# A hybrid attention and state-space layer on one core: the states' scans in two steps, their rotation back on GpSimd, the phasors as two rows with the third negated by ScalarE

## The chip, the cores and the metric

The kernel runs on 1 core of one Trainium2 chip. The metric is device microseconds from start to end of one execution, the median of several runs. Engines are named as the profile names them: PE is TensorE (matmul; PEld its weight loads), DVE is VectorE, ACT is ScalarE, POOL is GpSimd, SP is SyncE, which issues most DMAs here.

## The reference

One layer on 2048 positions of width 1024, in float32. Two branches share one input projection: latent attention (4 heads), and a bidirectional S5 state-space branch, 32 groups of 16 channels with 64 complex states in each direction. The part that matters here, cut:

```python
lam_bar = jnp.exp(lam * dt)
b_bar = ((lam_bar - 1.0) / lam)[..., None] * b
bu = jnp.einsum('sbgh,gph->sbgp', u_c, b_bar)
a = jnp.broadcast_to(lam_bar, (seq, 1, SSM_GROUPS, SSM_STATE))
_, h = lax.associative_scan(_diag_scan_op, (a, bu), reverse=reverse, axis=0)
y = y + jnp.real(jnp.einsum('sbgp,ghp->sbgh', h, c))
...
s = jnp.einsum('bqhd,bkhd->bhqk', qn, k_nope) + jnp.einsum('bqhr,bkr->bhqk', qr, k_rope)
p = jax.nn.softmax(s * scale, axis=-1)
return jnp.einsum('bhqk,bkhd->bqhd', p, v)
```

After that: GELU and a gated linear unit on the S5 branch, a norm and a gate on both, one output projection, a norm and the residual.

## The kernel before

Phase 1 projects the input, phase 3 does the output side. Between them lies the attention phase, in which all of S5 runs too; the change touches that phase alone. It is one hand-written loop (`for t in range(8 * NU + LAG + AVLAG + 3)`) of 256 steps with scores and a short tail. All five engines are scheduled by hand: each engine executes its instructions in exactly the order in which this loop emits them, and an instruction that waits holds everything behind it on its engine.

One step of attention: five score matmuls of 512 columns (L1103 to L1107, into `sc`, two PSUM buffers); the row maximum `nm` on DVE (L1108); the exponential `e` on ACT (L1114); the scaling of an older `e` on ACT (`norm`, L1143); four transposes of an older `e` on PE (`pt`, L1151), split into `phi` on ACT (L1159) and `plo` on DVE (L1573); and six matmuls with the values on the `phi` and `plo` of the step before (`av`, L1171 to L1173). Every eight steps a unit (128-query pairs, one head) ends, with some small statistics on DVE.

S5 runs group by group: `group(g)` is a generator that does one piece before and one after the attention's part of each step. A new group starts every 7 steps (twice 6), and each takes 15, so that two or three are under way. In this text a **round** is the 7 steps from the start of one group, and **offsets** 0 to 6 count its steps. At offset o the new group does its step o, and the group before it does its step 7 + o; of step 14, at offset 0, there is the older one's end. By a group's own steps, before the change:

- steps 0 and 1: the table `w` on POOL (L905, L906, L961). Step 2: `t3`, the phasors over the chunks as three rows (-sin, cos, sin), as two products on POOL, `t` and `t3b` (L971, L972); step 3: their sum (L975), then transposes of `w` on PE, split by ACT and DVE (`wTh`, `wTl`).
- step 5: matmuls `px`. Step 6: `ta` and `tb` on DVE from `px` and the phasors (L996, L997). Step 7 (offset 0 of the next round): `X`, their sum (L1001).
- step 8 (offset 1): four scans on DVE, real and imaginary part, forward and backward (L1008, L1009), from `X` into `G`.
- step 9 (offset 2): the rotation back: `hc`, a product on DVE (L1017), and `tb2`, shown as `tb`, a product on POOL (L1018).
- step 10 (offset 3): their difference, again `hc`, on DVE (L1021).
- step 14 (offset 0): `hc` goes into matmuls.

What shares POOL's queue in a round: three instructions of a table `v` for a later four groups (L905, L906, L915), in some rounds a split of inputs (`ul` L883, `ml` L889, which wait for ACT), and `qd` of the next queries (L750), which waits for DVE.

Of the kernel before, what the change touches and what calls it, by code (L numbers as in the profile page):

```python
# [11 lines left out]
F32 = mybir.dt.float32  # L12
# [4 lines left out]
ALU = mybir.AluOpType  # L17
# [4 lines left out]
P = 128  # L22
# [34 lines left out]
class Metered:  # L57
    """An engine that counts the elements it is given."""
# [13 lines left out]
class Scratch:  # L72
    """Temporaries of one shape, out of a ring of tiles of 512 (or, if small, 32) elements."""
# [10 lines left out]
def reduce_angle(eng, sc, out, ang):  # L84
    """out = ang - 2 pi round(ang / 2 pi)."""
    k = sc()
    eng.tensor_scalar(k, ang, 1.0 / TWO_PI, MAGIC, ALU.mult, ALU.add)
    eng.tensor_scalar(k, k, MAGIC, None, ALU.subtract)
    yield
    eng.scalar_tensor_tensor(out, k, -PI_1, ang, ALU.mult, ALU.add)  # L90
    for c in (PI_2, PI_3, PI_4):
        yield
        eng.scalar_tensor_tensor(out, k, -c, out, ALU.mult, ALU.add)
    yield


def sincos(eng, sc, sin_out, cos_out, r):
    """sin and cos of r in about [-pi, pi], from those of r / 2."""
    z, a = sc(), sc()
    eng.scalar_tensor_tensor(z, r, 0.25, r, ALU.mult, ALU.mult)  # L100
    s = [(-1.0) ** n / math.factorial(2 * n + 1) for n in range(1, 7)]
    eng.tensor_scalar(a, z, s[5], None, ALU.mult)
    for c in s[4::-1]:
        yield
        eng.scalar_tensor_tensor(a, a, c, z, ALU.add, ALU.mult)
    yield
    s2 = sc()
    eng.scalar_tensor_tensor(s2, a, 1.0, r, ALU.add, ALU.mult)
    c = [(-1.0) ** n / math.factorial(2 * n) for n in range(1, 8)]
    eng.tensor_scalar(a, z, c[6], None, ALU.mult)  # L110
    for v in c[5::-1]:
        yield
        eng.scalar_tensor_tensor(a, a, v, z, ALU.add, ALU.mult)
    yield
    eng.scalar_tensor_tensor(sin_out, a, 1.0, s2, ALU.add, ALU.mult)
    yield
    eng.scalar_tensor_tensor(cos_out, s2, -0.5, s2, ALU.mult, ALU.mult)
    eng.tensor_scalar(cos_out, cos_out, 1.0, None, ALU.add)
    yield


def exp_of(eng, sc, pool, out, x):
    """exp(x) in float32, exact at 0."""
    xc, n, r, a = sc(), sc(), sc(), sc()
    eng.tensor_scalar(xc, x, -87.0, 88.0, ALU.max, ALU.min)
    eng.tensor_scalar(n, xc, 1.0 / math.log(2.0), MAGIC, ALU.mult, ALU.add)
    eng.tensor_scalar(n, n, MAGIC, None, ALU.subtract)
    eng.scalar_tensor_tensor(r, n, -LN2_1, xc, ALU.mult, ALU.add)
    eng.scalar_tensor_tensor(r, n, -LN2_2, r, ALU.mult, ALU.add)
    yield  # L130
    eng.tensor_scalar(a, r, 1.0 / 5040, None, ALU.mult)
    for k in (720, 120, 24, 6, 2, 1):
        eng.scalar_tensor_tensor(a, a, 1.0 / k, r, ALU.add, ALU.mult)
    eng.tensor_scalar(a, a, 1.0, None, ALU.add)
    yield
    e = pool.tile(sc.shape, I32, tag="expi", name="expi")
    eng.tensor_scalar(n, n, 127.0, None, ALU.add)
    eng.tensor_copy(e, n)
    eng.tensor_scalar(e, e, 23, None, ALU.logical_shift_left)
    eng.tensor_tensor(out, a, f32(e), ALU.mult)  # L140


def bc(ap, dims):
    return ap.to_broadcast(dims)
# [3 lines left out]
def tile_hymba(ctx, tc, x, pos, inv_freq, pre_g, w_in, q_g, w_uqT, w_uqr, kv_g, w_ukT, w_uv, attn_g,  # L148
# [35 lines left out]
    def rsqrt_of(ss, n, scale, eps=EPS):  # L184
        """(ss * scale + eps) ** -0.5 on [128, n]."""
        v = sm.tile([P, n], F32, tag=f"rv{n}", name="rv")
        r = sm.tile([P, n], F32, tag=f"rr{n}", name="rr")
        V.tensor_scalar(v, ss, scale, eps, ALU.mult, ALU.add)
        G.tensor_tensor(r, v, nhalf[:, :n], ALU.pow)
        return r  # L190

    def split(hi, lo, src, scale=None):
        """hi + lo = src (* a scale for each partition), both float32r."""
# [12 lines left out]
    # tables of the attention phase; those of S5 go through DRAM, by groups  # L206
# [11 lines left out]
    # ------------------------------------------------------------------ phase 1  # L218
# [51 lines left out]
    def turn(xt, t):  # L270
        """The tile's transpose, split, as tile t of a pair."""
# [34 lines left out]
    def gemm_t(nm, half):  # L306
        """Two blocks of 128 columns of a pair of tiles, with the columns in the partitions."""
# [43 lines left out]
    def s5_params():  # L351
# [37 lines left out]
        # F = (lam_bar - 1) / lam  # L389
# [17 lines left out]
        # powers of lam_bar, 0 .. T, in the order of each direction  # L407
# [29 lines left out]
        # phasors of chunk 32 i + 2 j + a: ph32 * (0..7) (+ phi), for a = 0, 1, and ph2 * (0..15)  # L437
# [13 lines left out]
        for nm, src in (("b", ph2), ("a", ph32)):  # L451
# [21 lines left out]
            # the backward direction turns the other way  # L473
# [11 lines left out]
        # B_bar = F B; B'' = B_bar e^{-i phi}; C' = lam_bar C  # L485
# [3 lines left out]
        def cm(orr, oi, ar, ai, xr_, xi_):  # L489
            """(orr, oi) = (ar + i ai)(xr + i xi), a over the last dimension."""  # L490
# [32 lines left out]
        # centre lag: Re(C B_bar) of both directions + D  # L523
        # (eight groups at a time: theirs are the blocks on the diagonal)
# [36 lines left out]
    def step():  # L561
        """A slice of the tables, of about BUDGET elements."""
# [4 lines left out]
    def blocks(s):  # L567
        """The columns of two tiles, a block of columns at a time: z goes first and last, tile by tile,
        so that the next tiles can take the places of these meanwhile."""
# [8 lines left out]
    # absorbed weights: W_uq[h] W_uk[h]^T  # L578
# [23 lines left out]
    # the first tile is loaded and normed by halves  # L602
# [48 lines left out]
    # ------------------------------------------------------------------ phase 2  # L651
    # (the gate columns of the last two tiles run under its start)
# [43 lines left out]
    # queries of a block of 256: each piece's last results are split a step later  # L696
# [74 lines left out]
    def both(*gens):  # L771
        """Step some routines in turn; what each returns."""
# [14 lines left out]
    # the gate columns of the last two tiles run under the start of the attention  # L787
# [58 lines left out]
    # S5  # L846
# [8 lines left out]
    def s5_load(q):  # L855
        """The tables of four groups."""
# [34 lines left out]
    def ops4(tile_, q_r, q_i, c1, c2):  # L891
        """The operands of tile_[., 2, s, h] = q_r[s] c1[., h] + q_i[s] c2[., h]."""
# [9 lines left out]
    def two(eng, tile_, tmp, *o):  # L902
        """The two products of a table; later they are added."""
# [18 lines left out]
    def k_build(q):  # L922
        """The kernels of the lags within a chunk, and their windows for each position."""
# [26 lines left out]
    def group(g):  # L950
        """A group of channels, a step at a time: what is ready first, what needs the PE last."""
        q, i = divmod(g, 4)
        f = S5[q]
        # (chunks in the order of their tiles: those of the even, then those of the odd places)
# [9 lines left out]
        # phasors over the chunks: -sin, cos, sin  # L964
        t3 = s2.tile([P, 3, 16, 16], F32, tag="t3", name="t3", bufs=2)
        t3b = s2.tile([P, 3, 16, 16], F32, tag="t3b", name="t3b")
        d = [P, 3, 16, 16]
# [3 lines left out]
        G.tensor_tensor(t3, bc(f["aa"][:, i, 1:4, :].unsqueeze(3), d), b4(f["bc"]), ALU.mult)  # L971
        G.tensor_tensor(t3b, bc(f["aa"][:, i, 0:3, :].unsqueeze(3), d), b4(f["bs"]), ALU.mult)  # L972
        yield "pre"
        yield "post"
        G.tensor_tensor(t3, t3, t3b, ALU.add)  # L975
# [7 lines left out]
        yield "post"  # L983
        yield "pre"
# [19 lines left out]
        # (the states that enter the chunks; nothing enters the first, or the last backwards)  # L1004
# [6 lines left out]
        yield "pre"  # L1011
        yield "post"
# [4 lines left out]
        V.tensor_tensor(of_tiles(hc), g4, co, ALU.mult)  # L1017
# [3 lines left out]
        V.tensor_tensor(hc, hc, tb2, ALU.subtract)  # L1021
        yield "pre"
        yield "post"
# [20 lines left out]
    # when each group starts; the tables of the next four groups are made meanwhile  # L1044
# [52 lines left out]
    # attention  # L1097
# [19 lines left out]
    # the blocks of a row were shifted by their own maxima: bring them to the row's, and divide  # L1117
# [67 lines left out]
    # ------------------------------------------------------------------ weights of phase 3  # L1185
# [52 lines left out]
    # ------------------------------------------------------------------ phase 3  # L1238
    # (pairs of tiles, with the channels in the partitions up to W_out)
    def mixer():  # L1240
# [26 lines left out]
        def gelu(d):  # L1267
            """y <- 2 gelu(y), and its parts"""
# [38 lines left out]
        def part(d, src, h, c):  # L1307
            """hi and lo of half h of src, as blocks c .. of the products' operands"""
# [16 lines left out]
        def summed(d, sq):  # L1325
            """The sums of squares of the four channels in a partition"""
# [5 lines left out]
        def attn(d):  # L1332
            """o gated, and its parts"""
# [16 lines left out]
        def ssm(d):  # L1350
            """y <- 4 y sigmoid(. + b), gated into g, and its parts"""
# [37 lines left out]
        # the columns of the result in the parts that are worked on; the last tile ends in smaller ones  # L1389
# [11 lines left out]
        def comb(d, t, cs):  # L1401
            """Both branches by their factors, summed; the mean of the squares; times the gain"""
# [40 lines left out]
        # the first pairs, in small steps between those of the attention  # L1443
# [103 lines left out]
    for t in range(8 * NU + LAG + AVLAG + 3):  # L1547
        n, i = divmod(t, 8)
        # what the step before has made ready
# [5 lines left out]
        # scores  # L1555
# [23 lines left out]
        # (without scores in between, its operands take a step longer)  # L1579
# [8 lines left out]
        # the queries of the next block  # L1588
# [37 lines left out]
def layout(i):  # L1626
    """The inputs, laid out for the core; nothing is computed from them."""
# [51 lines left out]
```

## Time and profile before

| | before |
|---|---|
| median of 3 runs | 1433.84 us (1433.35 to 1434.98) |
| span of the profiled execution | 1431.5 us |
| PE, DVE, ACT, POOL busy | 95%, 74%, 55%, 44% |
| PE granted clock, mean | 0.997 |

The span runs from the first to the last instruction in one profiled execution; the median lies 2.3 us above it. Busy shares are over the whole span. The attention phase is the middle of it: its first score matmul starts at 394 us, its last step's at 1168 us. PE is pipelined and the ends of its matmuls are modelled, so that busy PE time may hide short waits.

### The profile page before, as it was taken

How to read it: one execution, taken by the hardware profiler on the slowest of the kernel's cores; microseconds unless marked ns; L12 is line 12 of the kernel's file. 1: busy time of each engine (PE TensorE's matmuls, PEld its weight loads, DVE VectorE, ACT ScalarE, POOL GpSimd, SP SyncE). 2: the span in 40 equal slices, each digit the busy share in tenths (PEclk: the TensorE clock that was granted, in tenths of full speed). 3: DMA queues.
4: the chain of work that ended last, by engine and by line, in shares of the span. 5: the costliest groups of instructions: out<-in, count | busy, mean ns of one | idle time of the engine just before them, and what ended most of it. 6: DMA issues, size and time to landing. Idle time of an engine off the chain costs nothing.

```text
span 1431.5 us, 24291 instructions
## 1 busy us (share of the span) xinstructions
PE 1359.6 (95%) x9016; PEld 1221.6 (85%) x9016; DVE 1053.7 (74%) x1876; ACT 789.0 (55%) x1796; POOL 624.9 (44%) x616
## 2 busy tenths in 40 slices
PE   7999999999989999999999998999999989999998
PEld 7999999999968788887888887887888878788886
DVE  5456545332588888898989888988888895876774
ACT  6321222122457767767677676676677775544542
POOL 2102321233364655555556555645542695323340
PEclk9999999999999999999999999999999999999999
DMA  8322332442610110201102011020100345345432
GB/s 293 89 61 66 80 87 73 98 122 73 150 35 19 39 34 5 54 19 31 41 5 61 12 32 41 23 43 5 32 5 9 101 128 131 118 148 179 145 103 88
DMA packets 122133, 102.91 MB, mean 72 GB/s; under 512 B 14672, under 2 KB 107104, under 8 KB 122016
## 3 DMA queue, kind: packets, MB, share of 16 engines
q1 hardware_dynamic: 110384, 89.43, 22.3%
q0 software_dynamic: 2272, 7.62, 2.0%
q10 hardware_dynamic: 9360, 4.33, 1.5%
q8 instruction: 70, 1.15, 0.3%
q14 instruction: 47, 0.39, 0.1%
HBM read 63.80 MB, written 37.54 MB: 71 GB/s over the span
## 4 chain that ended last, share of the span: by engine, by line
PE 59%; DVE 26%; ACT 5%; issue 4%; POOL 2%; DMA 2%; SPq 1%; ACTq 0%; POOLq 0%; DVEq 0%
DVE plo L1573 5%; DVE nm L1108 4%; PE po L202 4%; PE po L203 4%; PE po L204 4%; PE pt L1151 3%; DVE hc L1017 3%; DVE G L1009 3%; DVE G L1008 3%; PE z_ga L203 2%; PE z_ga L204 2%; PE z_ga L202 2%; PE av L1173 2%; PE z_u L204 2%; PE z_u L202 2%
## 5 line engine op out<-in xcount | busy, mean ns | idle before, releaser
L1114 ACT ACTIVATE e<-sc,nm 128x512 f32<-128x512 f32 x256 | 176.4, 689 | 141.1 <-DVE nm L1108 139.8
L1573 DVE TENSOR_TENSOR plo<-pt,phi 128x512 fp32r<-128x512 f32 x255 | 175.0, 686 | 49.2 <-ACT phi L1159 46.3
L1159 ACT ACTIVATE phi<-pt 128x512 fp32r<-128x512 f32 x256 | 152.8, 597 | 72.9 <-PE pt L1151 72.4
L1108 DVE TENSOR_REDUCE nm<-sc 128x1 f32<-128x512 f32 x256 | 175.0, 683 | 17.6 <-PE sc L1107 15.6
L1173 PE MATMUL av<-plo,kn_h 128*128 128x256 f32 x512 | 150.6, 294 | 30.0 <-DVE plo L1573 29.5
L1171 PE MATMUL av<-phi,kn_h 128*128 128x256 f32 x512 | 165.7, 324 | 13.3 <-ACT avs L1176 13.2
L1143 ACT ACTIVATE e<-e,f 128x512 f32<-128x512 f32 x226 | 163.8, 725 | 1.5 <-DVE f L1132 1.5
L1151 PEld LDWEIGHTS pt<-ident,e 128*128 128x128 f32 x1024 | 127.8, 141 | 38.9 <-DVE e L1139 4.5
L1151 PE MATMUL pt<-ident,e 128*128 128x128 f32 x1024 | 154.8, 274 | 4.3 <-DVE e L1139 3.5
L1172 PE MATMUL av<-phi,kn_l 128*128 128x256 f32 x512 | 144.6, 282 | 0.0
L1173 PEld LDWEIGHTS av<-plo,kn_h 128*128 128x128 f32 x512 | 96.5, 189 | 40.1 <-DVE plo L1573 39.3
L1018 POOL TENSOR_TENSOR tb<-G,t 128x512 f32<-128x512 f32 x32 | 41.6, 1301 | 192.2 <-DVE G L1009 192.2
L1103 PE MATMUL sc<-kT_h,qo 128*128 128x512 f32 x256 | 114.7, 448 | 2.9 <-ACT e L1114 1.4
L1171 PEld LDWEIGHTS av<-phi,kn_h 128*128 128x128 f32 x512 | 97.6, 191 | 16.6 <-ACT avs L1176 16.5
L202 PE MATMUL po<-woh,ah 128*128 128x512 f32 (+1 forms) x264 | 102.6, 389 | 1.9 <-ACT u L1410 1.9
L203 PE MATMUL po<-wol,ah 128*128 128x512 f32 (+1 forms) x264 | 102.4, 388 | 0.0
L204 PE MATMUL po<-woh,al 128*128 128x512 f32 (+1 forms) x264 | 102.3, 388 | 0.0
L1104 PE MATMUL sc<-kT_l,qo 128*128 128x512 f32 x256 | 101.5, 396 | 0.0
L1106 PE MATMUL sc<-krS,qo 128*128 128x512 f32 x256 | 101.3, 396 | 0.0
L1107 PE MATMUL sc<-krS,qo 128*128 128x512 f32 x256 | 101.2, 395 | 0.0
L1105 PE MATMUL sc<-kT_h,qo 128*128 128x512 f32 x256 | 100.8, 394 | 0.0
L1172 PEld LDWEIGHTS av<-phi,kn_l 128*128 128x128 f32 x512 | 97.7, 191 | 0.0
(337 smaller groups left out, 4148.6 us busy)
## 6 DMA issues: line engine op xcount, KB each, us to landing
g_d<-gst SPq DMA_DIRECT2D x64, 128.0 KB, 2.0
g<-g_d SPq DMA_DIRECT2D x16, 512.0 KB, 5.7
xr<-in_x_dram SPq DMA_DIRECT2D x16, 512.0 KB, 6.7
xt<-in_x_dram SPq DMA_DIRECT2D x15, 512.0 KB, 3.8
out_dram<-res SPq DMA_DIRECT2D x15, 512.0 KB, 3.1
u_d<-ust ACTq DMA_DIRECT2D x64, 64.0 KB, 2.1
u<-u_d SPq DMA_DIRECT2D x64, 64.0 KB, 2.5
o_d<-o SPq DMA_DIRECT2D x32, 128.0 KB, 1.8
```

The costliest lines, as they stand in the source:

```text
L202: PE.matmul(ps, ahi, bhi, start=first, stop=False)
L203: PE.matmul(ps, ahi, blo, start=False, stop=False)
L204: PE.matmul(ps, alo, bhi, start=False, stop=last)
L1108: V.tensor_reduce(st["nm"][:, qt, kb:kb + 1], ps, AX.X, ALU.max, negate=True)
L1114: A.activation(e, st.pop("s"), AF.Exp, bias=st["nm"][:, qt, kb:kb + 1], accum_out=st["L"][:, qt, kb:kb + 1])
L1143: A.activation(e, e, AF.Copy, scale=f)
L1151: PE.transpose(pt[:, kk, qt, :], st["e"][qt, kt // 4][:, o:o + P], ident)
L1159: A.activation(hi, ptf, AF.Copy)
L1171: PE.matmul(o, kn_h[:, kt, :], hi[:, w], start=kt == 0, stop=False)
L1172: PE.matmul(o, kn_l[:, kt, :], hi[:, w], start=False, stop=False)
L1173: PE.matmul(o, kn_h[:, kt, :], lo[:, w], start=False, stop=kt == NT - 1)
L1573: V.tensor_tensor(lo[0], lo[1], f32(lo[2]), ALU.subtract)
```

## The change

In `group(g)` alone (docstrings and comments are also gone, which moves the line numbers; after the rotation back they are lower by one):

```diff
-        t3b = s2.tile([P, 3, 16, 16], F32, tag="t3b", name="t3b")
-        d = [P, 3, 16, 16]
+        t3b = s2.tile([P, 2, 16, 16], F32, tag="t3b", name="t3b")
+        d = [P, 2, 16, 16]
...
-        G.tensor_tensor(t3, bc(f["aa"][:, i, 1:4, :].unsqueeze(3), d), b4(f["bc"]), ALU.mult)
-        G.tensor_tensor(t3b, bc(f["aa"][:, i, 0:3, :].unsqueeze(3), d), b4(f["bs"]), ALU.mult)
+        G.tensor_tensor(t3[:, 0:2], bc(f["aa"][:, i, 1:3, :].unsqueeze(3), d), b4(f["bc"]), ALU.mult)
+        G.tensor_tensor(t3b, bc(f["aa"][:, i, 0:2, :].unsqueeze(3), d), b4(f["bs"]), ALU.mult)
         yield "pre"
         yield "post"
-        G.tensor_tensor(t3, t3, t3b, ALU.add)
+        G.tensor_tensor(t3[:, 0:2], t3[:, 0:2], t3b, ALU.add)
...
         split(wh_, wl_, pw[:, 0:256])
         yield "post"
+        A.activation(t3[:, 2, :], t3[:, 0, :], AF.Copy, scale=-1.0)
         yield "pre"
...
             V.tensor_tensor_scan(gt[64:P, o + 1:o + NC][:, ::-1], df[64:P], xm[64:P, r, 1:][:, ::-1], 0.0,
                                  ALU.mult, ALU.add)
-        yield "pre"
-        yield "post"
+            yield "pre"
+            yield "post"
...
-        V.tensor_tensor(of_tiles(hc), g4, co, ALU.mult)
+        G.tensor_tensor(of_tiles(hc), g4, co, ALU.mult)
         G.tensor_tensor(of_tiles(tb2), g4[:, ::-1], si, ALU.mult)
         yield "pre"
         yield "post"
-        V.tensor_tensor(hc, hc, tb2, ALU.subtract)
-        yield "pre"
-        yield "post"
+        G.tensor_tensor(hc, hc, tb2, ALU.subtract)
```

So the scans of the real part stay at step 8 and those of the imaginary part move to step 9; the rotation back moves from steps 9 and 10 to steps 10 and 11, all of it on POOL; one pair of empty yields goes, so that steps 12 to 14 stay where they were. The phasors' products have 512 elements in a partition, not 768, and ACT writes the third row at step 4.

Where this stands in the queues. First DVE, one round in the middle of the phase, from the `nm` and `plo` of offset 0 on (`G` is what the scans write; the numbers behind names tell buffers apart); before:

```order
L1108 TENSOR_REDUCE nm<-sc 128x1
L1573 TENSOR_TENSOR plo<-pt_9349,phi 128x512
L1008 SCALAR_TENSOR_TENSOR G_4637<-tab_7930,X_4639 64x255
L1009 SCALAR_TENSOR_TENSOR G_4637<-tab_7930,X_4639 64x255
L1008 SCALAR_TENSOR_TENSOR G_4637<-tab_7930,X_4639 64x255
L1009 SCALAR_TENSOR_TENSOR G_4637<-tab_7930,X_4639 64x255
L1108 TENSOR_REDUCE nm<-sc 128x1
L1573 TENSOR_TENSOR plo<-pt_9391,phi 128x512
L1017 TENSOR_TENSOR hc<-G_4637,t_9140 128x512
L1108 TENSOR_REDUCE nm<-sc 128x1
L1573 TENSOR_TENSOR plo<-pt_9426,phi 128x512
L1021 TENSOR_TENSOR hc<-hc,tb_9412 128x512
```

and the same round with the change:

```order
L1107 TENSOR_REDUCE nm<-sc 128x1
L1572 TENSOR_TENSOR plo<-pt_9366,phi 128x512
L1009 SCALAR_TENSOR_TENSOR G_4637<-tab_7942,X_4639 64x255
L1010 SCALAR_TENSOR_TENSOR G_4637<-tab_7942,X_4639 64x255
L1107 TENSOR_REDUCE nm<-sc 128x1
L1572 TENSOR_TENSOR plo<-pt_9406,phi 128x512
L1009 SCALAR_TENSOR_TENSOR G_4637<-tab_7942,X_4639 64x255
L1010 SCALAR_TENSOR_TENSOR G_4637<-tab_7942,X_4639 64x255
L1107 TENSOR_REDUCE nm<-sc 128x1
L1572 TENSOR_TENSOR plo<-pt_9439,phi 128x512
```

Two scans now stand between one `nm` and the next where there were four, and both `hc` are gone from this queue. Second POOL, from the table `w` of a new group to the end of the older group's rotation; before:

```order
L905 TENSOR_TENSOR w<-tab_7930 128x256
L906 TENSOR_TENSOR tmp<-tab_7930 128x256
L961 TENSOR_TENSOR w<-w,tmp 128x256
L1018 TENSOR_TENSOR tb_9137<-G_4638,t_8842 128x512
L971 TENSOR_TENSOR t_9140<-tab_7930 128x768
L972 TENSOR_TENSOR t3b<-tab_7930 128x768
L975 TENSOR_TENSOR t_9140<-t_9140,t3b 128x768
```

and with the change:

```order
L905 TENSOR_TENSOR w<-tab_7942 128x256
L906 TENSOR_TENSOR tmp<-tab_7942 128x256
L961 TENSOR_TENSOR w<-w,tmp 128x256
L971 TENSOR_TENSOR t_9152<-tab_7942 128x512
L972 TENSOR_TENSOR t3b<-tab_7942 128x512
L1018 TENSOR_TENSOR hc<-G_4638,t_8853 128x512
L1019 TENSOR_TENSOR tb_9191<-G_4638,t_8853 128x512
L975 TENSOR_TENSOR t_9152<-t_9152,t3b 128x512
L1022 TENSOR_TENSOR hc<-hc,tb_9191 128x512
```

The first instruction that needs the scans' result `G` stood ahead of the new group's phasors; now the two products of the phasors stand ahead of it, and behind it come one more product and one difference. Third ACT, where the negation comes in (a later group), with the change:

```order
L195 ACTIVATE wTh<-pw_10354 128x256
L1142 ACTIVATE e<-e,f 128x512
L984 ACTIVATE t_10287<-t_10287 128x256
L1158 ACTIVATE phi<-pt_10371 128x512
L1113 ACTIVATE e,L<-sc,nm 128x512
```

The row of L984 is new; it stands between the scaling of `e` and `phi` of offset 4, and it reads what POOL's sum (L975) wrote.

## Rows read from the trace of the kernel before

**Rows 1.** The page: span, and busy time of each engine over it.
```profile
span 1431.5 us, 24291 instructions
...
PE 1359.6 (95%) x9016; PEld 1221.6 (85%) x9016; DVE 1053.7 (74%) x1876; ACT 789.0 (55%) x1796; POOL 624.9 (44%) x616
```

**Rows 2.** The page: the chain of waits that ended last, shares by engine.
```profile
PE 59%; DVE 26%; ACT 5%; issue 4%; POOL 2%; DMA 2%; SPq 1%; ACTq 0%; POOLq 0%; DVEq 0%
```

**Rows 3.** Busy time by stretch: offsets 2 to 4 of 31 rounds, and their sum.
```profile
core 0: us, PE busy (x) PEld busy (x) DVE busy (x) ACT busy (x) POOL busy (x), PEclk, DMA share, GB/s
...
577.13:584.74 7.61, 7.59 (x50) 6.58 (x48) 7.15 (x10) 5.84 (x14) 7.53 (x6) 1.00 0.35 95
...
642.10:652.55 10.45, 8.12 (x53) 6.81 (x51) 9.59 (x15) 6.59 (x18) 6.51 (x4) 1.00 0.01 2
...
708.33:717.03 8.70, 8.14 (x55) 7.14 (x54) 7.98 (x17) 5.42 (x14) 6.77 (x5) 1.00 0.01 2
...
839.59:847.40 7.81, 7.81 (x54) 6.91 (x53) 6.83 (x11) 5.92 (x17) 7.73 (x6) 1.00 0.36 92
...
sum 295.50, PE 255.45 PEld 218.74 DVE 269.84 ACT 192.85 POOL 240.18; mean PE 8.24 PEld 7.06 DVE 8.70 ACT 6.22 POOL 7.75
```

**Rows 4.** The same for the four other offsets of these rounds, summed.
```profile
sum 380.10, PE 378.72 PEld 337.90 DVE 328.00 ACT 285.71 POOL 129.41; mean PE 12.22 PEld 10.90 DVE 10.58 ACT 9.22 POOL 4.17
```

**Rows 5.** Groups on DVE: count, busy us, mean ns, idle before and releaser.
```profile
L1017 DVE TENSOR_TENSOR hc<-G,t 128x512 f32<-128x512 f32 x32 | 52.3, 1635 | 0.0
L1009 DVE TENSOR_TENSOR_SCAN G<-tab,X 64x255 f32<-64x255 f32 x64 | 46.3, 724 | 0.9
L1008 DVE TENSOR_TENSOR_SCAN G<-tab,X 64x255 f32<-64x255 f32 x64 | 45.4, 709 | 0.4
L1021 DVE TENSOR_TENSOR hc<-hc,tb 128x512 f32<-128x512 f32 x32 | 41.3, 1292 | 2.5 <-POOL tb L1018 2.5
```

**Rows 6.** Timeline of DVE, 641 to 650 us: start, us, instruction.
```profile
641.83 0.69 DVE L1009 TENSOR_TENSOR_SCAN G<-tab,X 64x255 f32<-64x255 f32 x1
...
643.88 2.03 DVE L1017 TENSOR_TENSOR hc<-G,t 128x512 f32<-128x512 f32 x1
...
647.83 1.92 DVE L1021 TENSOR_TENSOR hc<-hc,tb 128x512 f32<-128x512 f32 x1
```

**Rows 7.** Timeline of POOL, the same stretch.
```profile
642.60 1.31 POOL L1018 TENSOR_TENSOR tb<-G,t 128x512 f32<-128x512 f32 x1 [10.71 <-DVE G L1009]
...
647.34 1.85 POOL L975 TENSOR_TENSOR t<-t,t3b 128x768 f32<-128x768 f32 x1
```

**Rows 8.** Timeline of DVE in another round: the product with POOL idle at its start.
```profile
710.02 0.68 DVE L1017 TENSOR_TENSOR hc<-G,t 128x512 f32<-128x512 f32 x1
```

**Rows 9.** Timeline of PE, the stretch of rows 6: idle before an instruction, and its releaser.
```profile
647.16 0.39 PE L1173 MATMUL av<-plo,kn_h 128*128 128x256 f32 x1 [0.58 <-DVE plo L1573]
...
651.48 0.39 PE L1171 MATMUL av<-phi,kn_h 128*128 128x256 f32 x1 [1.75 <-ACT avs L1176]
```

**Rows 10.** Groups on POOL.
```profile
L975 POOL TENSOR_TENSOR t<-t,t3b 128x768 f32<-128x768 f32 x32 | 63.1, 1971 | 2.2
L972 POOL TENSOR_TENSOR t3b<-tab 128x768 f32<-128x768 f32 x32 | 60.3, 1885 | 0.0
L971 POOL TENSOR_TENSOR t<-tab 128x768 f32<-128x768 f32 x32 | 48.1, 1502 | 0.0
L1018 POOL TENSOR_TENSOR tb<-G,t 128x512 f32<-128x512 f32 x32 | 41.6, 1301 | 192.2 <-DVE G L1009 192.2
```

**Rows 11.** Groups on ACT: a copy of 128x256.
```profile
L195 ACT ACTIVATE wTh<-pw 128x256 fp32r<-128x256 f32 x32 | 12.3, 384 | 0.0
```

**Rows 12.** Timeline of DVE, POOL and ACT, the round of the first stretch of rows 3.
```profile
576.30 0.69 DVE L1009 TENSOR_TENSOR_SCAN G<-tab,X 64x255 f32<-64x255 f32 x1
...
581.82 2.17 POOL L975 TENSOR_TENSOR t<-t,t3b 128x768 f32<-128x768 f32 x1
...
583.86 0.72 ACT L1143 ACTIVATE e<-e,f 128x512 f32<-128x512 f32 x1
```

**Rows 13.** Timeline of DVE and POOL, a round in which POOL's splits came late.
```profile
506.78 1.61 DVE L1009 TENSOR_TENSOR_SCAN G<-tab,X 64x255 f32<-64x255 f32 x1
...
507.80 1.69 POOL L889 TENSOR_TENSOR ml<-m,mh 128x512 fp32r<-128x512 f32 x1
```

## The prediction

> **What bounds the kernel now.** I read the page first: over the span of 1431.5 us PE is busy for 1359.6, DVE for 1053.7, POOL for 624.9 [rows 1]. PE looks like the bound; but the chain of waits lies on DVE for 26% [rows 2], so somewhere PE waits for DVE, and the question is where. The change touches the attention phase alone, so I cut that phase by rounds and asked for busy time by stretch: offsets 2 to 4, three steps that hold the rotation back, against the four other offsets, for 31 rounds. The reader should see how different the two are. Offsets 2 to 4 last 295.5 us in all with PE busy for 255.45: 40.05 us of idle PE, 1.29 a round, with DVE busy 91% and POOL 81% of it [rows 3]. The other four offsets last 380.10 us with PE busy for 378.72: 1.38 us of idle in all, POOL busy 34% [rows 4]. So nearly all the visible idle time of PE in S5's rounds sits just behind the scans.
>
> The timeline of one such round tells why. The last scan ends at 642.52 [rows 6]; only then can POOL start `tb`, the first instruction that reads the scans' result, after 10.71 us of idling, and then it runs its queue without a break until 649.19 (647.34 + 1.85) [rows 7]. DVE's own two products of that rotation fall into that burst: `hc` takes 2.03 us and the difference 1.92 [rows 6], where the same product with POOL idle at its start takes 0.68 [rows 8]. The 2.03 is close to `tb`'s 1.31 plus 0.68: DVE seems to wait until POOL's instruction is done. Over all groups they average 1635 and 1292 ns [rows 5]. Everything behind them on DVE is late, `plo` above all, and PE shows it: 0.58 us before `av` for `plo`, and 1.75 for `avs`, which itself waits for those `av` [rows 9].
>
> **The change part by part.** *The rotation leaves DVE.* Removed: 32 products and 32 differences, 52.3 + 41.3 = 93.6 us of busy DVE, 2.93 a round [rows 5]. Nothing comes in their place there. Offsets 2 to 4 had 8.70 us of busy DVE in 9.53 us [rows 3]; without 2.93 and with the two scans that move in (0.709 + 0.724 [rows 5]) it is 7.2.
>
> *The scans in two steps.* Four scans, 2 x (709 + 724) = 2.87 us [rows 5], stood in one block ahead of an `nm`; now it is twice 1.43, with an `nm` and a `plo` between. The sum of DVE's work is the same, but no row maximum waits for more than two scans. The last scan ends later by one `nm` and one `plo`, some 1.4 us.
>
> *POOL.* The phasors: 1502 + 1885 + 1971 = 5.36 us a round for 768 elements [rows 10]. For 512, two thirds of it is 3.57; at the 1301 ns of `tb`, which has 512, it is 3.90; I take 3.7, since the nearest row has its size. Added: a product and a difference of 512 elements, 2 x 1.30 = 2.60. Sum: +0.94 us a round, 30 us in all. POOL is busy for (240.18 + 129.41) / 31 = 11.9 us of a round of 21.8 [rows 3, 4], so that there is room; cost nothing, hidden by POOL's idle time, as long as its queue is not late at the negation (below).
>
> What these products cost by engine: 0.68 us on DVE undisturbed [rows 8], 1.30 on POOL [rows 10]. The Trainium skill, "GPSIMD Engine Reference", section "Engine selection", says that elementwise work belongs on VectorE, GpSimd being about twice as slow with two inputs. If the rotation set the round's length, that rule would cost 2 x 0.62 x 32 = 40 us here. But `hc` is read only at step 14, three steps after its difference, some 8 us (three steps have 8.24 us of PE's work [rows 3]); so I take nothing for it.
>
> *ACT.* 32 copies of 128x256 at 384 ns [rows 11], 12.3 us, on an engine busy for (192.85 + 285.71) / 31 = 15.4 us of 21.8 [rows 3, 4]. The cost is the wait, not the work: ACT's queue stands behind POOL's sum of the phasors. In the round of rows 12 the last scan ended at 576.99 and that sum at 583.99, 7.00 us later, while ACT came to the scaling of `e` at 583.86 and would reach the negation at 584.58: 0.6 us to spare [rows 12]. With the change `hc`, `tb` and the sum stand behind the scans, 3 x 1.30 = 3.9 us in place of 7.0, and the scans end 1.4 later: 1.7 us earlier in sum, while the steps get shorter by about as much as PE's idle (1.29 over three steps). The margin holds, if the phasors' two products have run before the scans are done. They need only the table, so that POOL can do them in the idle time that it now has at the scans (10.71 us [rows 7]), unless something ahead of them waits. In 15 of 30 rounds something does stand between: `ml` in 8, which waits for ACT, and `qd` in 10, which waits for DVE (3 have both).
>
> *The sum.* In the free half of the rounds I expect the idle 1.29 to go, and a little of what hides in busy PE: the stretch at 839.59 has no idle and lasts 7.81, with as many matmuls (54) as the one at 708.33 with 8.14 of busy PE [rows 3]. That is 1.29 + 0.25 = 1.54, by 16 rounds 25 us. In the other half POOL still meets DVE's scans; such a collision makes a scan 1.61 us, 0.9 more [rows 13]. I take half the gain: 0.75 x 15 = 11. Sum -36 us, the span from 1431.5 to 1395.5. The median of the runs is 2.3 us above that execution's span, so I forecast 1397.8, say 1398 us.
>
> **The rivals.** *1. Slower: POOL is late in every round and holds ACT and DVE.* Place: the two phasor products run behind `ml` and `qd` and into the scans. Each of four scans then takes up to 0.92 us more (1.61 against 0.69, rows 13 and 6), 3.7 a round, more than the 2.93 that were taken away; DVE has 0.75 more, times 32 is 24 us, and the span would be 1456, the median 1458. It decides once the phasors' sum ends over about 1 us behind ACT's arrival at the negation, which then holds `phi` and `e` as well. For it: the collision is there [rows 13], and the negation adds a wait that was not there. Against: POOL idled 10.71 us before the scans' result [rows 7]. Chance 0.10. The Trainium skill, "SBUF — State Buffer", section "Who interferes with whom", says that a VectorE instruction with two SBUF inputs and a GpSimd one that reads SBUF exclude each other for a whole instruction, and whoever starts first holds the other up. By that rule, more work on POOL is more delay for the scans, which speaks against the change; the trace agrees on the mechanism (2.03 for 1.31 + 0.68), and it is the same rule by which the removal of `hc` from DVE gains.
>
> *2. DVE's time is freed, but PE does not wait for it.* The stretch at 708.33 had both products undisturbed (the first is in rows 8) and still lasted 8.70 with 0.56 idle [rows 3]: latency from ACT and the small statistics stays. If all rounds only come down from 9.53 to about 9.0, with the collisions at the scans left, the gain is 0.5 x 32 = 16 us or less: the median at 1418 or above. Chance 0.22, of which 0.06 for no change at all, when the new waits eat that too.
>
> *3. All rounds like the best.* Every stretch at 7.81: (9.53 - 7.81) x 32 = 55 us, the median at 1379. For it: POOL's burst meets nothing but reads from PSUM afterwards. Chance 0.12.
>
> *4. The change does not do what it says.* The orders show that it moves what it names; no chance of its own.
>
> **How the numbers follow.** Forecast 0.56 (gains of 16 to 50 us), rival 3 0.12, rival 2 0.22, rival 1 0.10. The range 1374 to 1422 takes in rival 3 with 5 us of further hidden waits, and rival 2 down to a gain of 12; what lies above is rival 1 and the part of rival 2 that gains less. About 0.2%, 3 us, is what a measurement of this kernel tells from no change: faster 0.84, within it 0.06, slower 0.10.
>
> **What would show it.** In the profile after: `hc` gone from DVE's groups and on POOL at about 1.3 us each; the scans in pairs, most at 0.7; in offsets 2 to 4 idle PE at a third of 1.29 a round or less, and DVE busy for about 7.2 us of them; POOL's phasor products before the scans' end in the free rounds, the idle time of POOL now before `hc`. Wrong, if ACT's groups show idle time before the negation for POOL's sum of more than some 15 us in all; if the scans average over 1 us; or if PE's idle time stays and is now put down to `phi`.

## The result, and the profile after

The changed kernel takes 1394.19 us in the median (1393.85 to 1395.39, 4 runs), the kernel before 1433.59 in the same comparison: a ratio of 0.9725, 95% interval 0.9711 to 0.9739. It is 39.4 us faster; 1398 was forecast, with a range of 1374 to 1422. The span of the profiled execution fell by 37.9 us.

The page of the changed kernel, its span, busy times and chain, as in [rows 1, 2]:

```profile
span 1393.6 us, 24338 instructions
...
PE 1352.6 (97%) x9016; PEld 1220.4 (88%) x9016; DVE 980.2 (70%) x1812; ACT 799.3 (57%) x1828; POOL 644.6 (46%) x680
...
PE 76%; DVE 11%; ACT 4%; POOL 3%; issue 3%; DMA 2%; SPq 1%; POOLq 0%; DVEq 0%; ACTq 0%
```

PE does the same work; DVE's share of the chain went from 26% to 11%, and PE's from 59% to 76%. Busy time by stretch, summed over offsets 2 to 4 of the same 31 rounds, and then over the four other offsets (they answer to [rows 3, 4]; stretch, then busy us by engine):

```profile
sum 258.19, PE 246.91 PEld 216.94 DVE 215.77 ACT 202.37 POOL 184.34; mean PE 7.96 PEld 7.00 DVE 6.96 ACT 6.53 POOL 5.95
...
sum 379.69, PE 378.68 PEld 337.21 DVE 310.52 ACT 286.64 POOL 203.73; mean PE 12.22 PEld 10.88 DVE 10.02 ACT 9.25 POOL 6.57
```

All of the gain lies where the prediction put it: offsets 2 to 4 went from 295.50 to 258.19 us, 37.3 less, and the others stayed (380.10 and 379.69). Idle PE there fell from 40.05 to 11.28 us. The other 8.5 us came out of busy PE (255.45 to 246.91, with no fewer matmuls: 1667 records against 1661), which had hidden short waits.

Groups on DVE, POOL and ACT of the changed kernel (count, busy us, mean ns, idle before and releaser), against [rows 5, 10, 11]:

```profile
L1010 DVE TENSOR_TENSOR_SCAN G<-tab,X 64x255 f32<-64x255 f32 x64 | 53.7, 839 | 0.9
L1009 DVE TENSOR_TENSOR_SCAN G<-tab,X 64x255 f32<-64x255 f32 x64 | 46.7, 730 | 0.0
```

```profile
L1019 POOL TENSOR_TENSOR tb<-G,t 128x512 f32<-128x512 f32 x32 | 41.8, 1307 | 0.0
L1018 POOL TENSOR_TENSOR hc<-G,t 128x512 f32<-128x512 f32 x32 | 41.7, 1303 | 157.2 <-DVE G L1010 105.7 <-PE pt L1150 51.5
L975 POOL TENSOR_TENSOR t<-t,t3b 128x512 f32<-128x512 f32 x32 | 41.5, 1298 | 0.2
L1022 POOL TENSOR_TENSOR hc<-hc,tb 128x512 f32<-128x512 f32 x32 | 41.4, 1293 | 0.6
L971 POOL TENSOR_TENSOR t<-tab 128x512 f32<-128x512 f32 x32 | 39.5, 1235 | 0.0
L972 POOL TENSOR_TENSOR t3b<-tab 128x512 f32<-128x512 f32 x32 | 36.6, 1145 | 0.0
```

```profile
L984 ACT ACTIVATE t<-t 128x256 f32<-128x256 f32 x32 | 13.6, 424 | 6.4 <-POOL t L975 6.4
```

Both `hc` are on POOL at 1.3 us and gone from DVE. Of the scans, the second of each pair (L1010) meets POOL a little, in both steps: 53.7 us where there were 46.3; the first (L1009) has 46.7 where there were 45.4. The negation waited for POOL in four rounds, 6.4 us in all. Round by round, 17 of the 31 have no scan over 0.8 us; they gained 23.6 us at offsets 2 to 4, and 0.5 us of idle PE is left in them. The other 14, in which at least one scan was held up, gained 13.8 and keep 10.8 of the 11.28 us that are left. So the forecast came true; but the experiments show that one sentence on which it stood was wrong.

### The profile page after: what moved, and what is told of

Read it like the earlier page. It is cut to its first block, busy times and chain, and to the rows that moved or that the text cites. A ratio compares the mean times of both kernels' runs of the same rounds, so it can differ in the third digit from the quotient of the medians.

```text
span 1393.6 us, 24338 instructions
## 1 busy us (share of the span) xinstructions
PE 1352.6 (97%) x9016; PEld 1220.4 (88%) x9016; DVE 980.2 (70%) x1812; ACT 799.3 (57%) x1828; POOL 644.6 (46%) x680
## 4 chain that ended last, share of the span: by engine, by line
PE 76%; DVE 11%; ACT 4%; POOL 3%; issue 3%; DMA 2%; SPq 1%; POOLq 0%; DVEq 0%; ACTq 0%
PE pt L1150 5%; PE po L202 4%; PE po L204 4%; PE po L203 4%; PE av L1172 3%; PE sc L1102 3%; PE av L1170 3%; PE av L1171 3%; PE sc L1103 3%; PE sc L1105 3%; PE sc L1106 3%; PE sc L1104 3%; PE z_ga L203 2%; PE z_ga L204 2%; PE z_ga L202 2%
## 5 line engine op out<-in xcount | busy, mean ns | idle before, releaser
L1018 POOL TENSOR_TENSOR hc<-G,t 128x512 f32<-128x512 f32 x32 | 41.7, 1303 | 157.2 <-DVE G L1010 105.7
```

## The experiments

Theory R was the prediction's: what costs is that the rotation's two products on DVE are held up in POOL's burst, so moving them is the gain. Rival S: the block of four scans is what holds the rest up. Rival P: the length of POOL's burst is.

### One part at a time

**The scans alone:** the change without its phasors and with the rotation on VectorE.

```diff
-        G.tensor_tensor(of_tiles(hc), g4, co, ALU.mult)
+        V.tensor_tensor(of_tiles(hc), g4, co, ALU.mult)
...
-        G.tensor_tensor(hc, hc, tb2, ALU.subtract)
+        V.tensor_tensor(hc, hc, tb2, ALU.subtract)
```

with `t3` and `t3b` of three rows as before, and no negation.

> Against the kernel before, the scans alone stand in two steps (the rotation one step later, still on VectorE; three phasor rows on GpSimd, no negation). Theory R (the two products of the rotation on VectorE, held up by GpSimd's burst, made nearly all the loss): a small gain, 3 to 10 us, since both products still stand in VectorE's queue behind the scans and still meet GpSimd; they last over 1.2 us on the mean. Rival S (the block of four scans ahead of one row maximum made it): 20 us or more, idle PE at offsets 2 to 4 halved or less.

Measured: 1433.16 us, ratio 0.9997 (0.9983 to 1.001). No change at all, less than theory R gave it; rival S falls as it was stated. The zero is a gain and a loss. Offsets 2 to 4, and then the four others, against 295.50 and 380.10 before [rows 3, 4]:

```profile
sum 278.32, PE 251.31 PEld 216.90 DVE 254.99 ACT 189.21 POOL 174.61; mean PE 8.11 PEld 7.00 DVE 8.23 ACT 6.10 POOL 5.63
...
sum 396.72, PE 384.06 PEld 339.27 DVE 346.28 ACT 291.46 POOL 197.18; mean PE 12.39 PEld 10.94 DVE 11.17 ACT 9.40 POOL 6.36
```

With the rotation a step later, 17.2 us went from the first and 16.6 came to the others.

**The phasors alone:** scans in one step, rotation on VectorE a step earlier, both as before; two rows on GpSimd and the negation stay.

> Against the kernel before, the phasors alone are changed: two rows on GpSimd, the third negated by ScalarE. Theory R: GpSimd's instructions are shorter by a third, so that the difference on VectorE is held up less; the product is still held up by the whole of the other one (1.3 us). Gain 3 to 10 us. Rival P (the length of GpSimd's burst made it): 20 us or more. If the new wait of ScalarE for the phasors' sum hurts where the scans still stand in one block: slower by some us.

Measured: 1408.49 us, ratio 0.9819 (0.9797 to 0.984), a gain of 25 us. Theory R had given it 3 to 10.

**The rotation alone:** three phasor rows and scans in one step, as before; only the two lines of the diff above have GpSimd (`G`), as in the change.

> Against the kernel before, the rotation alone is changed: its product and difference on GpSimd, in the same steps as before; scans in one step, three phasor rows. Theory R: 25 us or more of the 39 us, 1400 to 1410 us; the scans stay at about 0.7 us, since GpSimd's queue still stands behind them; idle PE at offsets 2 to 4 falls to about half or less. Rival S: 10 us or less, with the idle time of PE still behind the block of scans.

Measured: 1404.95 us, ratio 0.9785 (0.9754 to 0.9815), 28 us. As theory R had it.

**The change without the rotation's move:** the two lines of that diff, and nothing else, on the changed kernel.

> The changed kernel with the rotation put back on VectorE (scans in two steps and two phasor rows stay). Theory R: most of the gain is lost, 1420 us or above. Rivals S and P: most of the gain stays, 1405 us or below.

Measured: 1402.11 us, ratio 0.9777 (0.9754 to 0.98). Theory R had 1420 or above; 31 of 39 us stay without the move. So theory R falls as it was stated: moving the rotation is enough for most of the gain, but not needed for it, and two parts that share no instruction (phasors, rotation) each bring most of it alone. That suggests that they cure the same thing in two ways.

What they cure shows in the groups. DVE of the kernel with the phasors alone, where `hc` and the difference still stand on DVE, in the same steps:

```profile
L1022 DVE TENSOR_TENSOR hc<-hc,tb 128x512 f32<-128x512 f32 x32 | 34.0, 1063 | 2.5 <-POOL tb L1019 2.5
L1018 DVE TENSOR_TENSOR hc<-G,t 128x512 f32<-128x512 f32 x32 | 26.2, 819 | 0.0
```

The product fell from 1635 ns [rows 5] to 819. If it had waited for `tb`, as the prediction said, it would not have: `tb` still takes 1.30 us. POOL's timeline of the kernel before, the stretch of [rows 7], with the row that was left out there (start, us, instruction):

```profile
643.87 1.50 POOL L971 TENSOR_TENSOR t<-tab 128x768 f32<-128x768 f32 x1
```

Against it stands DVE's `hc`, from 643.88 for 2.03 us [rows 6]. `tb` was done at 643.91, when `hc` had hardly begun. What held `hc` up was the next instruction, the new phasors' first product, which had started 0.01 us before it: until 645.37, and 0.54 us of `hc` came after that. Now POOL and DVE of the kernel with the phasors alone:

```profile
464.49 1.28 POOL L1019 TENSOR_TENSOR tb<-G,t 128x512 f32<-128x512 f32 x1 [10.88 <-DVE G L1010]
465.73 1.57 POOL L971 TENSOR_TENSOR t<-tab 128x512 f32<-128x512 f32 x1
```

```profile
463.66 0.69 DVE L1010 TENSOR_TENSOR_SCAN G<-tab,X 64x255 f32<-64x255 f32 x1
...
465.70 0.68 DVE L1018 TENSOR_TENSOR hc<-G,t 128x512 f32<-128x512 f32 x1
```

Here `hc` starts 0.03 us ahead, takes its 0.68, and POOL's product is the one that is held up (1.57, where it takes 1.06 in the rounds in which it starts first). The Trainium skill, "SBUF — State Buffer", "Who interferes with whom", says that of two such instructions the one that starts first holds the other up for its whole length; these two pairs agree, in both directions.

### Theory T: a tie, lost in 19 of 32 rounds

Both instructions follow the same event, the end of the last scan: POOL by `tb`, 1.30 us; DVE by `nm` and `plo`, some 1.3 us. In the timelines of the kernel before, the two start within 0.05 us of each other in 19 of 32 rounds, and POOL is first in all 19, by 0.003 to 0.045 us; `hc` lasts 2.00 us or more in each. In eight others it runs undisturbed, at 0.68. Why did the phasors' change turn that round? `tb` reads the third phasor row, which ACT now writes, so that it waits for ACT besides DVE. It started 0.08 us after the scan before ([row 641.83 of rows 6, row 642.60 of rows 7]: 642.52 to 642.60) and 0.14 us after it in the rows above (464.35 to 464.49).

**Tie:** the kernel before with one instruction more.

```diff
         G.tensor_tensor(of_tiles(tb2), g4[:, ::-1], si, ALU.mult)
+        G.memset(s2.tile([P, 1], F32, tag="pause", name="pause"), 0.0)
```

> The kernel before with one more instruction on GpSimd in each round: a memset of one column (some 0.1 us), between the rotation's product there and the first product of the next phasors. Nothing is taken away. Theory T (in the kernel before the phasors' product on GpSimd and the rotation's product on VectorE come ready within some 0.04 us of each other, GpSimd starts first in most rounds, and VectorE is then held up for the whole of it): VectorE now starts first, its product falls from 1.6 us to under 1.0 us on the mean, the time falls by 15 to 25 us, to 1408 to 1418 us. Rivals S and P, and theory R as first stated: no change or a little slower, 1431 to 1438 us.

Measured: 1413.57 us, ratio 0.9859 (0.9845 to 0.9874): 20 us faster for an added instruction that computes nothing. POOL and DVE, one round; the group; and offsets 2 to 4 summed:

```profile
463.20 1.30 POOL L1018 TENSOR_TENSOR tb<-G,t 128x512 f32<-128x512 f32 x1 [8.82 <-DVE G L1009]
...
464.44 0.10 POOL L1019 MEMSET pause<- 128x1 f32 x1
464.48 0.68 DVE L1017 TENSOR_TENSOR hc<-G,t 128x512 f32<-128x512 f32 x1
464.49 2.03 POOL L971 TENSOR_TENSOR t<-tab 128x768 f32<-128x768 f32 x1
...
L1017 DVE TENSOR_TENSOR hc<-G,t 128x512 f32<-128x512 f32 x32 | 25.3, 790 | 0.0
...
sum 276.04, PE 251.91 PEld 217.94 DVE 244.43 ACT 196.82 POOL 231.46; mean PE 8.13 PEld 7.03 DVE 7.88 ACT 6.35 POOL 7.47
```

`hc` now wins by 0.01 us: 0.68 for DVE and 2.03 for POOL, the reverse of [rows 6] and the row at 643.87. In 17 of the 19 rounds DVE is first; in two POOL's start is recorded 0.002 and 0.003 us ahead, and `hc` lasts 0.68 there too, so that at this distance the recorded starts do not tell who wins. Idle PE at offsets 2 to 4 falls from 40.05 to 24.13 us. This is theory T shown by itself: the tie costs the kernel before some 20 us.

**Wait only:** the kernel before with the negation added and nothing else (three rows of 768 still made on GpSimd, the third then written again).

```diff
         split(wh_, wl_, pw[:, 0:256])
         yield "post"
+        A.activation(t3[:, 2, :], t3[:, 0, :], AF.Copy, scale=-1.0)
```

> The kernel before with nothing but ScalarE's negation added: GpSimd still makes all three phasor rows of 768 elements, and ScalarE writes the third once more. Work is only added (13 us on ScalarE), but the rotation's product on GpSimd now waits for ScalarE as well as for the scans. Theory T: this second wait alone starts that product some 0.07 us later, as in the kernel with the phasors alone, so that the next one on GpSimd comes behind VectorE's product, which falls under 1.0 us; 1410 to 1420 us. Rival P (it was the shorter products): 1433 to 1440 us.

Measured: 1425.12 us, ratio 0.9946 (0.993 to 0.9962). The tie is turned (DVE first in 16 of the 19 rounds, the group below): in these 16 `tb` starts 0.14 us after the last scan, in the other three 0.08 as before, and there POOL is first. But the gain is 8.6 us, under the 14 to 24 that were expected.

```profile
L1018 DVE TENSOR_TENSOR hc<-G,t 128x512 f32<-128x512 f32 x32 | 29.3, 916 | 0.0
...
L984 ACT ACTIVATE t<-t 128x256 f32<-128x256 f32 x32 | 13.5, 421 | 6.9 <-POOL t L975 6.9
```

ACT has 13.5 us more to do and waits 6.9 us for a sum of 768 that comes late; that this is what eats the rest was not tried by itself. Between this kernel and the phasors alone (1408.49) lies only the length of POOL's three instructions, so that rival P has its part: some 16 us, once the tie is won.

**The scans alone, with the same memset:** the kernel of the first experiment with the line of the tie's diff.

> The kernel with the scans alone in two steps, and the same memset of one column on GpSimd behind the rotation's product. With the scans alone the product on VectorE still lost the tie (against the phasors' sum) in about a third of the rounds and fell into the midst of that sum in others. Theory T: 8 to 15 us faster than with the scans alone, 1418 to 1425 us; the product on VectorE falls from 1.75 to about 1.3 us on the mean. Rival: 1433 us, no change.

Measured: 1419.08 us, ratio 0.9899 (0.9884 to 0.9913), 14 us under the scans alone; `hc` 1130 ns where it had 1749. First with the scans alone, then with the memset:

```profile
L1017 DVE TENSOR_TENSOR hc<-G,t 128x512 f32<-128x512 f32 x32 | 56.0, 1749 | 0.0
...
L1017 DVE TENSOR_TENSOR hc<-G,t 128x512 f32<-128x512 f32 x32 | 36.2, 1130 | 0.0
```

So the scans in two steps brought nothing alone in good part because `hc` then met the phasors' sum in place of their first product.

### What each part is worth beside the others

**Without the phasors' part** (three rows of 768 on GpSimd, no negation; scans and rotation as in the change):

> The changed kernel with the three phasor rows put back on GpSimd and no negation on ScalarE (scans in two steps and rotation on GpSimd stay). With the rotation off VectorE there is no tie left to lose, so theory T gives nearly the changed kernel's time, 1394 to 1400 us; longer GpSimd instructions hold up the second pair of scans a little more. Rival P: 1410 us or more. If the negation held ScalarE up: faster than 1394 us.

Measured: 1403.35 us, ratio 0.9788 (0.9774 to 0.9803), between the 1394 to 1400 of theory T and rival P's 1410. The second scan of each pair takes 963 ns on the mean there, against 839 in the change:

```profile
L1009 DVE TENSOR_TENSOR_SCAN G<-tab,X 64x255 f32<-64x255 f32 x64 | 61.6, 963 | 0.9
```

**Without the scans' part** (four scans in one step, the rotation on GpSimd a step earlier):

> The changed kernel with the four scans put back into one step (rotation on GpSimd a step earlier; two phasor rows and the negation stay). Theory T with R: 1396 to 1404 us, as the block of four scans makes the row maximum wait 1.4 us longer but no scan meets GpSimd. Rival S: 1410 us or more.

Measured: 1406.97 us, ratio 0.981 (0.9796 to 0.9825), between the 1396 to 1404 of theory T with R and rival S's 1410. The scans are as in the kernel before, 724 and 709 ns, but ACT pays (below, with the four other offsets summed):

```profile
L984 ACT ACTIVATE t<-t 128x256 f32<-128x256 f32 x32 | 13.4, 420 | 19.7 <-POOL t L975 19.2
...
sum 387.22, PE 379.69 PEld 337.11 DVE 317.19 ACT 285.81 POOL 152.96; mean PE 12.25 PEld 10.87 DVE 10.23 ACT 9.22 POOL 4.93
```

With the scans in one step the phasors' products stand behind `hc` and `tb` in POOL's queue, as they stood behind `tb` before; their sum comes late and the negation holds ACT for 19.2 us, against 6.4 in the change. So the split is worth some 13 us there (1406.97 to 1394.19). In the profiled executions 7.5 us of it lie in the four other offsets (387.22 against 379.69), where PE is idle for 7.5 us against 1.0, and 3.0 in offsets 2 to 4. That fits the negation's wait, and so what the split lets POOL do before the scans end, which rival S did not name; it was not tried apart from the block of scans itself.

Taken out one at a time, the phasors' part costs some 9 us, the scans' 13 and the rotation's 8 (1402.11 above), 30 of the 39; alone they bring 25, 0 and 28.

**Early:** a version beyond the change. The phasors' products go into POOL's queue with the table `w`, and their sum with that table's sum.

```diff
         two(G, wt, tmp, f["qr"][:, i, ::-1], f["qi"][:, i, ::-1], f["bt"][:, i, 1:3, :], f["bt"][:, i, 0:2, :])
+        G.tensor_tensor(t3[:, 0:2], bc(f["aa"][:, i, 1:3, :].unsqueeze(3), d), b4(f["bc"]), ALU.mult)
+        G.tensor_tensor(t3b, bc(f["aa"][:, i, 0:2, :].unsqueeze(3), d), b4(f["bs"]), ALU.mult)
         yield "pre"
         yield "post"
         G.tensor_tensor(wt, wt, tmp, ALU.add)
+        G.tensor_tensor(t3[:, 0:2], t3[:, 0:2], t3b, ALU.add)
```

(Not shown: what these lines need, the tiles `t3` and `t3b` above all, moves up too; where the lines stood they are gone, their yields stay.)

> The changed kernel with the phasors made earlier on GpSimd: their two products with those of the table w (step 0), their sum with that table's sum (step 1). Nothing of them stands behind the scans any more, and the negation never waits. If what is left of the loss (11 us of idle PE at offsets 2 to 4, second scans of 0.84 us on the mean) comes from phasor products running into the scans: 3 to 8 us faster, 1386 to 1391 us, scans at about 0.72 us. If it comes from latency elsewhere: 1393 to 1396 us.

Measured: 1390.43 us, ratio 0.9693 (0.9676 to 0.9709). Since that is close to the changed kernel, both were run once more on one chip:

> The kernel with the phasors made earlier, once more, on the same chip as the changed kernel and in more rounds: 1388 to 1392 us, 3 to 5 us under the changed kernel, if what was seen between two chips holds; 1393 to 1395 us if it was the chip.

> The changed kernel itself, on the same chip as the one with the phasors made earlier: 1393 to 1396 us.

Measured: 1389.69 us (1389.31 to 1391.02) and 1395.33 us (1394.51 to 1396.05), ratios 0.9697 (0.9683 to 0.971) and 0.9734 (0.9721 to 0.9748). It beats the change by 5.6 us. But the expected sign, scans at about 0.72 us, did not come: they are no shorter. Groups on DVE and ACT of the early version (its last run):

```profile
L1009 DVE TENSOR_TENSOR_SCAN G<-tab,X 64x255 f32<-64x255 f32 x64 | 55.1, 861 | 0.9
...
L983 ACT ACTIVATE t<-t 128x256 f32<-128x256 f32 x32 | 13.6, 426 | 0.0
```

22 of the 128 scans last over 0.8 us, against 20 in the change, and the four of a round come to 3.20 us against 3.14. What went is ACT's wait for the sum, from 6.4 us to nothing; whether it is the cause of the 5.6 us was not tried by itself, and stays open.

## Why the prediction was right, point by point

- *Where the time goes: offsets 2 to 4.* Right, to the microsecond (37.3 of 37.9).
- *Why it goes there.* Wrong in one sentence: "DVE seems to wait until POOL's instruction is done", said of `tb`, since 2.03 is close to 1.31 + 0.68. That sum was a coincidence. DVE waited for the instruction behind `tb`, which starts 0.01 us ahead of `hc`; the row that would have shown it, 643.87, was in the timeline and was not set against `hc`'s start. Moving `hc` to POOL cures this whichever instruction it waited for, so the forecast of the whole held; that the move was the only cure did not, as the memset's 20 us and the phasors' 25 show.
- *The rotation leaves DVE, 2.93 us a round.* Right in effect: DVE has 6.96 us of work in these three steps, 7.2 forecast.
- *The scans in two steps, so that no maximum waits for more than two.* True, and worth nothing alone. Beside the other parts it is worth some 13 us, more than half of them at the other offsets; the likely place is POOL's queue, where the phasors' products run before the scans' result is there (shown as ACT's wait of 6.4 us against 19.2, not by itself). The prediction had this as its condition for ACT's margin, not as a gain.
- *POOL, +0.94 us a round, 30 us.* Phasors 3.7 forecast, (41.5 + 39.5 + 36.6) / 32 = 3.68 measured. With 2.60 for the product and the difference, as forecast, these rows rose by 29 us. Busy POOL rose by 19.7 only: some 5 us are other instructions there that got shorter (`qd` from 1451 to 1389 ns, `ul` from 1367 to 1298, and smaller ones), and the rest was not followed up.
- *ACT's margin at the negation.* Right: 6.4 us of waiting, in four rounds, under the 15 named as the limit; the copy took 424 ns, not 384 (the row that was taken reads PSUM and writes another type; what makes the difference was not tried). Rival 1 can be seen at work in one round, where `qd` and `ml` came late:

```profile
497.22 1.60 POOL L750 TENSOR_TENSOR qd<-ta,tb 128x512 f32<-128x512 f32 x1 [7.84 <-DVE tb L747]
...
497.74 1.62 DVE L1010 TENSOR_TENSOR_SCAN G<-tab,X 64x255 f32<-64x255 f32 x1
...
498.76 1.70 POOL L889 TENSOR_TENSOR ml<-m,mh 128x512 fp32r<-128x512 f32 x1
...
502.13 1.06 POOL L972 TENSOR_TENSOR t3b<-tab 128x512 f32<-128x512 f32 x1
...
502.13 1.61 DVE L1009 TENSOR_TENSOR_SCAN G<-tab,X 64x255 f32<-64x255 f32 x1
...
511.70 0.42 ACT L984 ACTIVATE t<-t 128x256 f32<-128x256 f32 x1 [2.56 <-POOL t L975]
```

  Scans at 1.6 us and ACT held for 2.56, as it was described; it stayed with such rounds. The scans end 0.54 and 0.55 us after `qd` (498.82) and `t3b` (503.19), so these held them up, and not `ml`. The same goes for the row of `ml` in [rows 13]: there too it is `qd` (until 507.85) that the scan waited for. The kernel before:

```profile
506.26 1.59 POOL L750 TENSOR_TENSOR qd<-ta,tb 128x512 f32<-128x512 f32 x1 [10.12 <-DVE tb L747]
```

- *The sum, -36.* Measured -37.9 in the span. The visible idle time gave 28.8 (40.05 - 11.28), less than the forecast took for it, 16 x 1.29 and half of that in 15 more rounds, 30; the hidden part gave 8.5, where some 6 was taken, 16 x 0.25 and half of that in 15 more. The 0.25 had a loose base: the two stretches that it was read from have 54 and 55 matmuls [rows 3], not 54 both. The split into halves came out: 25 in 16 free rounds and 11 in 15 others were forecast, 23.6 in 17 and 13.8 in 14 were measured.

## What to carry to other kernels

When two engines whose instructions hold each other up start from the same event, set their starts side by side in the timeline: a tie of a few hundredths of a microsecond can come out the same way in every round, and an instruction of 0.1 us in the right queue can be worth 20 us. Before work is moved off a loaded engine, ask what else would turn the order round; parts that each "bring 25 us" may be cures of one thing, and their gains do not add. And a duration that equals the sum of two others is no proof of what it waited for: look up what was running when it ended.

## What the runs showed of the hardware

A product of 128x512 on DVE with both inputs in SBUF lasts 0.68 us or 2.03 us, and a product of 128x768 on POOL 1.50 or 2.03, depending on which of them starts first, by as little as 0.01 us: the one that is second takes its own time, less 0.13 to 0.14 us, after the other's end. Scans on DVE are held up in the same way (0.69 us, or 1.6 behind `qd`). Row maxima, which read PSUM, and `plo`, which reads PSUM and `phi`, were not: none of either lasts over 0.70 us in the kernel before or in the changed one. A second semaphore to wait for, set five steps before, moved the start of `tb` by some 0.06 us, and the tie turned in just the 16 of 19 rounds in which it did.
